# Low parts of two output projections: from a VectorE subtraction to a ScalarE negation and an adding transfer

## The chip, the core and the metric

The kernel runs on one core of one Trainium2 chip. The metric is the device time of one execution in microseconds (us), the median of several runs. Its engines are TensorE (PE; its weight loads are listed apart as PEld), VectorE (DVE), ScalarE (ACT), GpSimd (POOL) and SyncE (SP), which here only issues transfers.

## The reference, cut to what matters

The reference is a decoder trunk of two layers over 512 tokens of 1024 features, in float32. Layer 0 mixes tokens with gated linear recurrences (HGRN2 and retention heads), layer 1 with sparse attention. Each layer then has a SwiGLU network:

```python
for layer in range(DEPTH):
    hn = rmsnorm(h, mix_norm[layer])
    if layer % 2 == 0:
        h = h + even_mixer(hn, ...)      # ends in  o @ even_w_out   (1024 x 1024)
    else:
        h = h + odd_mixer(hn, ...)       # ends in  out @ odd_w_out  (1024 x 1024)
    h = h + swiglu(rmsnorm(h, ffn_norm[layer]), ffn_w_gate_up[layer], ffn_w_down[layer])
return rmsnorm(h, final_norm)
```

The change touches the weights of the two products that end the mixers, `o @ even_w_out` and `out @ odd_w_out`.

## The kernel before, in words

Features lie on the 128 partitions and the 512 tokens along the free dimension. To multiply float32 numbers precisely, each operand is cut into a high part, rounded to the float32r type, and a low part, the rest. A product is then three matmuls into the same PSUM bank (`mm3`, L89 to L91): high by high, high by low, low by high, written `wh` with `xh`, `wh` with `xl`, `wl` with `xh` for a weight `w`.

A weight tile of 128 by 1024 is loaded by SP into one of three buffers `raw` (`load`). `split` treats it in two halves of 512 columns: ACT writes the rounded high part `wh` (L78), and DVE subtracts it from `raw` to give `wl` (L79). There are seven buffers for `wh` and seven for `wl`, each for half a tile, so a cast waits until PE has read the half of seven halves before. A `raw` buffer is free for the next load once both halves are cut.

`ffn` begins with the output projection of the mixer: eight tiles in the order `OUT_ORDER` (0, 4, 1, 5, 2, 6, 3, 7), each of 24 matmuls into a bank `ps_o`. When a tile is done, DVE adds it to the residual `h` (L286), `token_side` forms the sums and differences of the two token halves for a Strassen product and cuts them into high and low parts (names `xg`, `b1`, `b2`, `t1` to `t4`, `tr`; ACT casts at L214, DVE subtractions at L215), and `square` gathers the sum of squares (`sq`, `acc`, L120 and L121). Then come the seven products of the gate and up projections, which need both the token sides of all tiles and the cut sums of four weight blocks (`weight_side`: `sw`, `sh`, `sl`, L259 to L264). The copies `u` (L327, L330, L335) carry partial sums out of PSUM between these products. The first group of the network has no down projection to run between its products.

The order of instructions on each engine is made by the scheduler of the tile framework: it goes by the order of the code as priority and by modelled times. Each engine then takes its instructions strictly in that order, and waits on semaphores that the framework sets. The eight tiles' weights are cast and cut ahead of their use, as far as the buffers allow: in layer 0 during the last projections of the mixer, in layer 1 during the attention.

The change adds `weight_add` beside `weight`, and calls it in `ffn` where `ps_o` is computed.

Of the kernel before, what the change touches and what calls it, by code (L numbers as in the profile page):

```python
# [9 lines left out]
F32 = mybir.dt.float32  # L10
F32R = mybir.dt.float32r
U8 = mybir.dt.uint8
AF = mybir.ActivationFunctionType
ALU = mybir.AluOpType
# [3 lines left out]
P = 128  # L18
# [8 lines left out]
WS = 512  # L27
# [25 lines left out]
class Core:  # L53
# [17 lines left out]
    def split(self, raw, n, pool):  # L71
        nc = self.nc
        out = []
        for o in range(0, n, WS):
            m = min(WS, n - o)
            wh = self.wp.tile([P, WS], F32R, tag="wh", name="wh", bufs=7)
            wl = self.wp.tile([P, WS], F32R, tag="wl", name="wl", bufs=7)
            nc.scalar.copy(wh[:, :m], raw[:, o:o + m])  # L78
            (nc.gpsimd if pool else nc.vector).tensor_tensor(wl[:, :m], raw[:, o:o + m], wh.bitcast(F32)[:, :m],  # L79
                                                             ALU.subtract)  # L80
            out.append((wh, wl))
        return out

# [186 lines left out]
    def ffn(self, outs, w_out, gain, layer, next_gain):  # L270
        tc, nc, io, sp = self.tc, self.nc, self.io, self.sp
        with tc.tile_pool(name="fs", bufs=1) as fs, tc.tile_pool(name="fps", bufs=6, space=PSUM) as fps:
# [4 lines left out]
            for i, m in enumerate(OUT_ORDER):  # L277
                ps = self.bank(self.turn + 1 + i // 3, "ps_o") if i in BANK_OUT else \
                    fps.tile([P, T], F32, tag="gu", name="ps_o")
                w = self.weight(w_out[m])  # L280
                if i == BANK_OUT[1] and self.last is not None:
                    with tc.issue_after(self.last):
                        self.dense_t(ps, w, outs)
                else:
                    self.dense_t(ps, w, outs)
                nc.vector.tensor_tensor(self.h[m], ps, self.h[m], ALU.add)  # L286
                self.token_side(m, gain, kept, b)
                self.square(m, self.h[m], acc)
# [13 lines left out]
            out = []  # L302
# [14 lines left out]
            for size in GROUPS:  # L317
                hid = []
                for j in range(done, done + size):
# [30 lines left out]
                    if before:  # L350
                        n = KD // size
# [809 lines left out]
```

## Time and profile before

| what | value |
|---|---|
| median of 3 runs | 1310.82 us (1310.17 to 1310.92) |
| the profiled execution's own time | 1311.86 us |
| its span, first to last instruction | 1308.9 us |
| outside the span | 2.96 us |
| mean granted TensorE clock | 0.984 |
| busy: PE, PEld, DVE, ACT, POOL | 97%, 86%, 79%, 56%, 25% |
| output projection of layer 0 on PE | 241.7 to 287.6 us, overlapped at its start with the mixer's end |
| output projection of layer 1 on PE | 900.9 to 936.1 us for most of it; a first part is run within the attention |

The busy share of an engine is an average over stages with different limits. The times of the rows are in us from the start of the span. A busy PE is not PE at its peak, since the ends of its pipelined matmuls are modelled.

### The profile page before, as it was taken

The numbers are of one execution on the slowest core, as the hardware profiler recorded it, in microseconds if no ns is written. First come the engines' busy times: TensorE is split into PE (matmuls) and PEld (weight loads), VectorE is DVE, ScalarE is ACT, GpSimd is POOL, SyncE is SP. The second block draws the span as 40 slices with busy tenths as digits, with TensorE's granted clock in tenths as the row PEclk, the third lists the DMA queues.
The fourth block names the chain that finished last, engine by engine and source line by source line (L and its number), as shares of the span: only waits on it lengthen the run. The fifth ranks groups of instructions, "written<-read, shape, count | busy, mean of one in ns | idle before, by whom it ended". The sixth has DMA issues, their size and how long they took to land.

```text
span 1308.9 us, 21707 instructions
## 1 busy us (share of the span) xinstructions
PE 1270.2 (97%) x7846; PEld 1120.7 (86%) x7846; DVE 1028.2 (79%) x2027; ACT 731.7 (56%) x1587; POOL 332.0 (25%) x371
## 2 busy tenths in 40 slices
PE   9999999998999999999988999999989999999995
PEld 7888888888999999999877888887889999999984
DVE  7896764699998887876762789995989888878755
ACT  6655444675554444444554778895755444444444
POOL 3432431001121111111015666762012111111101
PEclk9999999999999999999997999999989999999998
DMA  7212212123233333332322211101223333333321
GB/s 262 84 65 75 72 65 65 65 81 101 85 109 109 107 106 100 100 97 88 104 90 93 78 52 52 44 18 34 85 81 125 105 97 98 97 101 102 105 57 64
DMA packets 44123, 115.10 MB, mean 88 GB/s; under 512 B 4913, under 2 KB 10481, under 8 KB 44017
## 3 DMA queue, kind: packets, MB, share of 16 engines
q1 hardware_dynamic: 43872, 113.69, 27.2%
q8 instruction: 61, 1.00, 0.3%
q14 instruction: 46, 0.37, 0.1%
q10 hardware_dynamic: 144, 0.04, 0.0%
HBM read 111.62 MB, written 2.10 MB: 87 GB/s over the span
## 4 chain that ended last, share of the span: by engine, by line
PE 60%; DVE 8%; issue 2%; DMA 2%; ACT 2%; POOL 1%; DVEq 0%; ACTq 0%; POOLq 0%
PE p L89 9%; PE p L90 9%; PE p L91 9%; PE ps_d L90 5%; PE ps_d L91 5%; PE ps_d L89 5%; DMA raw<-in_gu 2%; PE po L966 2%; PE pt L935 2%; PE ps_o L89 2%; PE ps_o L91 2%; PE ps_o L90 2%; DVE wl L79 1%; PE ps_q L89 1%; PE ps_q L90 1%
## 5 line engine op out<-in xcount | busy, mean ns | idle before, releaser
L78 ACT CAST wh<-raw 128x512 fp32r<-128x512 f32 (+2 forms) x356 | 212.8, 605 | 216.2 <-PE p L90 76.8
L79 DVE TENSOR_TENSOR wl<-raw,wh 128x512 fp32r<-128x512 f32 (+2 forms) x340 | 244.0, 723 | 43.2 <-ACT wh L78 42.1
L214 ACT CAST sh<-sw 128x512 fp32r<-128x512 f32 x176 | 107.6, 618 | 144.4 <-PE p L90 126.4
L341 POOL TENSOR_TENSOR s<-s,rstd 128x256 f32<-128x256 f32 x44 | 38.9, 884 | 510.9 <-DVE s L336 451.7
L215 DVE TENSOR_TENSOR sl<-sw,sh 128x512 fp32r<-128x512 f32 x176 | 146.3, 848 | 6.5 <-ACT sh L214 6.2
L90 PE MATMUL ps_d<-hl,wh 128*128 128x512 f32 x344 | 136.0, 395 | 0.4 <-DVE hl L348 0.2
L91 PE MATMUL ps_d<-hh,wl 128*128 128x512 f32 x344 | 135.6, 394 | 0.0
L89 PE MATMUL ps_d<-hh,wh 128*128 128x512 f32 x344 | 134.5, 396 | 0.6 <-ACT hh L347 0.5
L342 POOL TENSOR_TENSOR g<-g,rstd 128x512 f32<-128x512 f32 x42 | 70.9, 1689 | 138.2 <-DVE g L338 114.5
L259 DVE TENSOR_TENSOR sw<-raw 128x512 f32<-128x512 f32 x44 | 30.3, 689 | 65.3 <-DMA raw<-in_gu 65.2
L91 PEld LDWEIGHTS ps_d<-hh,wl 128*128 128x128 f32 x344 | 64.5, 188 | 14.9
L918 ACT ACTIVATE p<-p,mx 128x256 f32<-128x256 f32 (+3 forms) x128 | 71.6, 564 | 10.1 <-DVE mx L910 9.6
L90 PE MATMUL ps_e<-xl,wh 128*128 128x512 f32 x192 | 76.7, 401 | 0.5 <-DVE xl L109 0.5
L927 POOL TENSOR_SCALAR p<-p,sm 128x128 f32<-128x128 f32 (+3 forms) x128 | 68.6, 554 | 33.2 <-DVE sm L924 15.0
L89 PE MATMUL ps_e<-xh,wh 128*128 128x512 f32 x192 | 76.8, 403 | 0.2
L91 PE MATMUL ps_e<-xh,wl 128*128 128x512 f32 x192 | 76.6, 401 | 0.0
L90 PEld LDWEIGHTS ps_d<-hl,wh 128*128 128x128 f32 x344 | 64.7, 188 | 13.2 <-DVE hl L348 1.0
L89 PEld LDWEIGHTS ps_d<-hh,wh 128*128 128x128 f32 x344 | 64.2, 188 | 13.5 <-ACT hh L347 1.0
L910 DVE CUSTOM_DVE_ANT_0 p<-ps_s,bias 128x256 f32<-128x256 f32 (+3 forms) x128 | 59.0, 481 | 8.1 <-PE pt L935 4.9
L313 DVE TENSOR_TENSOR h<-ps_d,h 128x512 f32<-128x512 f32 x80 | 54.6, 682 | 6.5 <-PE ps_d L91 6.3
L343 ACT ACTIVATE g<-g 128x512 f32<-128x512 f32 x44 | 27.8, 632 | 53.1 <-POOL g L342 52.9
L950 DVE TENSOR_TENSOR pl<-pt,ph 128x512 fp32r<-128x512 f32 (+2 forms) x96 | 51.5, 549 | 5.9 <-ACT ph L942 5.7
(342 smaller groups left out, 4112.8 us busy)
## 6 DMA issues: line engine op xcount, KB each, us to landing
raw<-in_gu SPq DMA_DIRECT2D x88, 512.0 KB, 3.8
raw<-in_dn SPq DMA_DIRECT2D x80, 256.0 KB, 2.7
raw<-in_ein SPq DMA_DIRECT2D x22, 512.0 KB, 3.7
raw<-in_oin SPq DMA_DIRECT2D x12, 512.0 KB, 3.7
raw<-in_eout SPq DMA_DIRECT2D x8, 512.0 KB, 3.8
bias<-in_bias SPq DMA_DIRECT2D x16, 256.0 KB, 2.6
raw<-in_oout SPq DMA_DIRECT2D x8, 512.0 KB, 3.5
h<-in_x SPq DMA_DIRECT2D x8, 256.0 KB, 5.0
```

The lines of the kernel that those rows point to most:

```text
L78: nc.scalar.copy(wh[:, :m], raw[:, o:o + m])
L79: (nc.gpsimd if pool else nc.vector).tensor_tensor(wl[:, :m], raw[:, o:o + m], wh.bitcast(F32)[:, :m], ALU.subtract)
L89: mm(ps, ah, bh, start=start, stop=False, skip_group_check=more)
L90: mm(ps, ah, bl, start=False, stop=False, skip_group_check=more)
L91: return mm(ps, al, bh, start=False, stop=stop, skip_group_check=more)
L214: nc.scalar.copy(hi, src)
L215: nc.vector.tensor_tensor(lo, src, hi.bitcast(F32), ALU.subtract)
L313: nc.vector.tensor_tensor(self.h[m], ps, self.h[m], ALU.add)
L342: (nc.vector if j == NF - 1 else nc.gpsimd).tensor_tensor(g, g, r, ALU.mult)
L910: nc.vector.tensor_tensor_reduce(p, h["dst"][:, b - br[0]], h["bias"][:, T - n:], -1.0, 3e38, ALU.add, ALU.min, h["mx"][:, t, b:b + 1])
L918: nc.scalar.activation(p, p, AF.Exp, bias=h["mx"][:, t, b:b + 1], scale=-1.0, accum_out=h["sm"][:, t, b:b + 1])
L927: nc.gpsimd.tensor_scalar(p, p, h["sm"][:, t, b:b + 1], 1.0, ALU.mult, ALU.mult)
```

## The change

For the sixteen weight tiles of the two output projections, in each of the 32 halves, DVE no longer subtracts. ACT casts the high part as before, then writes minus the high part into `wl`, and POOL issues a transfer from SBUF to SBUF that adds `raw` to `wl` in place. `wl` ends with the same value, raw minus high part.

```diff
+    def weight_add(self, ap):
+        nc = self.nc
+        n = ap.shape[1]
+        raw = self.load(ap)
+        out = []
+        for o in range(0, n, WS):
+            m = min(WS, n - o)
+            wh = self.wp.tile([P, WS], F32R, tag="wh", name="wh", bufs=7)
+            wl = self.wp.tile([P, WS], F32R, tag="wl", name="wl", bufs=7)
+            nc.scalar.copy(wh[:, :m], raw[:, o:o + m])
+            nc.scalar.activation(wl[:, :m], wh.bitcast(F32)[:, :m], AF.Identity, scale=-1.0)
+            nc.gpsimd.dma_start(wl.bitcast(F32)[:, :m], raw[:, o:o + m], accum_op=ALU.add)
+            out.append((wh, wl))
+        return out
...
-                w = self.weight(w_out[m])
+                w = self.weight_add(w_out[m])
```

## Rows read from the trace of the kernel before

**Rows 1.** Page, part 1: busy us (share of the span) xinstructions, by engine.

```profile
PE 1270.2 (97%) x7846; PEld 1120.7 (86%) x7846; DVE 1028.2 (79%) x2027; ACT 731.7 (56%) x1587; POOL 332.0 (25%) x371
```

**Rows 2.** Windows around layer 0's output projection: length, busy by engine, PEclk, DMA.

```profile
261.00:287.00 26.00, 26.00 (x113) 20.92 (x113) 25.98 (x53) 20.87 (x44) 0.00 (x0) 1.00 0.30 100
287.00:310.00 23.00, 18.92 (x129) 17.07 (x128) 22.97 (x49) 12.95 (x29) 0.36 (x1) 0.93 0.21 63
```

**Rows 3.** Windows in layer 1: attention, output projection, start of the network.

```profile
732.00:840.00 108.00, 107.49 (x660) 90.93 (x658) 96.28 (x326) 91.41 (x265) 79.22 (x118) 1.00 0.17 52
...
909.00:918.00 9.00, 9.00 (x41) 7.23 (x40) 8.96 (x20) 7.76 (x17) 0.00 (x0) 1.00 0.33 115
...
943.00:962.00 19.00, 14.54 (x85) 12.84 (x84) 15.58 (x32) 11.99 (x24) 0.73 (x1) 0.82 0.23 77
```

**Rows 4.** Waits of PE, 240 to 310 us: total, times, longest.

```profile
PE p L90 <- DVE t1l L215: 1.0, 1, 1.0
PE p L89 <- ACT u L335: 0.9, 1, 0.9
```

**Rows 5.** Group of ACT by form: busy us, mean ns of one, idle before it.

```profile
L108 ACT ACTIVATE xh<-h,par 128x512 fp32r<-128x512 f32 x16 | 11.3, 721 | 3.2 <-DMA par<-in_par 1.7 <-DMA h<-in_x 1.0 <-PE ps_d L91 0.6
```

**Rows 6.** Transfers by line: count, KB each, median us from issue to landing.

```profile
raw<-in_eout SPq DMA_DIRECT2D x8, 512.0 KB, 3.8
bias<-in_bias SPq DMA_DIRECT2D x16, 256.0 KB, 2.6
...
dec<-in_dec SPq DMA_DIRECT2D x1, 514.0 KB, 6.0
```

**Rows 7.** Timeline of DVE: start us, us, line, operation, out<-in.

```profile
261.62 0.68 DVE L79 TENSOR_TENSOR wl<-raw,wh 128x512 fp32r<-128x512 f32 x1
...
271.25 0.68 DVE L79 TENSOR_TENSOR wl<-raw,wh 128x512 fp32r<-128x512 f32 x1
...
273.40 0.68 DVE L259 TENSOR_TENSOR sw<-raw 128x512 f32<-128x512 f32 x1
...
290.06 0.68 DVE L286 TENSOR_TENSOR h<-ps_o,h 128x512 f32<-128x512 f32 x1
...
912.20 0.68 DVE L79 TENSOR_TENSOR wl<-raw,wh 128x512 fp32r<-128x512 f32 x1
912.80 0.42 DVE L215 TENSOR_TENSOR t3l<-tr,t3h 128x256 fp32r<-128x256 f32 x1
...
917.49 0.68 DVE L79 TENSOR_TENSOR wl<-raw,wh 128x512 fp32r<-128x512 f32 x1
...
937.02 0.68 DVE L286 TENSOR_TENSOR h<-ps_o,h 128x512 f32<-128x512 f32 x1
...
963.68 2.39 DVE L215 TENSOR_TENSOR sl<-sw,sh 128x512 fp32r<-128x512 f32 x2
```

**Rows 8.** Timeline of PE in the two projections and just behind the first.

```profile
246.41 0.63 PE L91 MATMUL ps_o<-oh,wl 128*128 128x512 f32 x2
...
271.08 0.40 PE L91 MATMUL ps_o<-oh,wl 128*128 128x512 f32 x1
...
287.18 0.39 PE L91 MATMUL ps_o<-oh,wl 128*128 128x512 f32 x1
...
288.72 0.28 PE L91 MATMUL p<-t1h,sl 128*128 128x256 f32 x1
...
935.68 0.40 PE L91 MATMUL ps_o<-oh,wl 128*128 128x512 f32 x1
```

**Rows 9.** Timeline of ACT, of SP's queue and of POOL.

```profile
242.09 0.64 ACT L78 CAST wh<-raw 128x512 fp32r<-128x512 f32 x1
...
260.55 1.66 ACT L78 CAST wh<-raw 128x512 fp32r<-128x512 f32 x3 [4.74 <-PE ps_o L90]
...
256.56 0.33 SPq L64 DMA_DIRECT2D raw<-in_eout  x1
...
963.25 1.68 POOL L342 TENSOR_TENSOR g<-g,rstd 128x512 f32<-128x512 f32 x1 [4.55 <-DVE g L338]
```

## The prediction

> **What bounds the kernel now.** I read the page's first part first: PE is busy for 1270.2 us of the span, DVE for 79% of it, ACT for 56%, POOL for 25% [rows 1]. So the time is PE's work plus PE's gaps, and the change takes no work off PE. It can only move gaps. The second view is therefore the windows, to find where PE has gaps near the weights that change, and the third is PE's list of waits there. In layer 0, PE is full from 261 to 287 us, while DVE is too, with 25.98 of 26 us. Then from 287 to 310 us PE is busy for only 18.92 of 23 us while DVE still has no free moment (22.97), and the granted clock averages 0.93 [rows 2]. In layer 1 the same stretch, 943 to 962 us, has PE busy for 14.54 of 19 us at a mean clock of 0.82 [rows 3]. These are gaps of 4.1 and 4.5 us. A mean of 0.93 over 23 us, with levels of 2.4 and 1.2 GHz, means 3.2 us at the lower level, which lose 1.6 us; 0.82 over 19 us means 6.8 us, which lose 3.4 us. So there is at most 4.1 + 1.6 = 5.7 us to get back behind the first projection, and 4.5 + 3.4 = 7.9 us behind the second.
>
> What sets these gaps? PE waits for both kinds of work: 1.0 us for a low part that DVE writes, 0.9 us for a copy that ACT makes between two products [rows 4]. How far DVE lags can be measured at the eighth tile. Its last matmul in layer 0 starts at 287.18 us and lasts 0.39 us [rows 8], but DVE adds the tile to `h` only at 290.06 us [rows 7]: 2.5 us late. In layer 1 the last matmul ends at 935.68 + 0.40 = 936.08 us [rows 8] and the add is at 937.02 us [rows 7]: 0.9 us late. So DVE carries a backlog into the stretch where PE starves, more in layer 0 than in layer 1.
>
> **What is removed.** 32 subtractions of 0.68 us [rows 7], 21.8 us of DVE's busy time. Neighbours overlap: the one at 912.20 us is followed at 912.80 us [rows 7], so each takes 0.60 us of DVE's queue, 19.2 us in all. Only those count that stand in a backlog that PE later feels. In layer 0 that is those from 261.62 to 271.25 us, six of them; in layer 1 those from 912.20 to 917.49 us, four [rows 7]. DVE's queue becomes shorter by 6 x 0.60 = 3.6 us and 4 x 0.60 = 2.4 us. It can't gain more than the lag, because then it waits for PE's tile. I take the smaller of the two each time: 2.5 us and 0.9 us, together 3.4 us. The lower bound is 0, if ACT's copies are what PE waits for; the upper bound is 6.0 us plus the 5.0 us of the slow clock.
>
> **What is added on ACT.** 32 negations from `wh` to `wl`. The nearest row of the same kind, an activation that writes float32r, takes 0.72 us [rows 5]; three casts in a row take 1.66 us, 0.55 us each [rows 9]. So ACT gets 18 to 23 us more. Around the projections there is room: 20.87 of 26 us and then 12.95 of 23 us are busy [rows 2]. In the attention there is little: 91.41 of 108 us [rows 3], and eight of the 32 halves are cut in that window. If all eight stood on the path, that would cost 8 x 0.72 = 5.8 us; DVE loses eight subtractions there, up to 4.8 us to the good. PE is busy for 107.49 of the 108 us, so little of either can reach it. I take +0.4 us.
>
> **What is added on POOL and as transfers.** The trace has no transfer issued by POOL and none that adds, so its cost is bounded. The issue takes between 0.33 us, as on SP's queue, and 1.68 us, POOL's own longest common instruction on a tile of this width [rows 9]; I take 1.0. The landing takes between 2.6 us (256 KB, plain) and 6.0 us (514 KB, the slowest load) [rows 6]. An adding transfer reads two tiles of 256 KB, so I take the 3.8 us of the 512 KB loads [rows 6]. The way from the end of the cast to a finished `wl` is then 0.7 + 1.0 + 3.8 = 5.5 us, with ends of 3.5 and 8.4 us. Now the same way is short: the first of the three casts at 260.55 us [rows 9] ends by 261.17 us, and its `wl` is done at 261.62 + 0.68 = 262.30 us [rows 7], 1.1 us later. So each low part comes about 4.4 us later than now, up to 7.3.
>
> Does PE notice? In the order of the code these casts are those of the sixth tile and of half the seventh. A tile is 24 matmuls at 0.233 us, 5.6 us, and the eighth ends at 287.18 us, so the sixth begins at 270.6 us; its first use of `wl` is the row at 271.08 us [rows 8]. The lead is 271.08 - 262.30 = 8.8 us. That is the shortest lead among the steady tiles of both layers, and even the upper end of 7.3 us fits. Only the tile that fills PE while the last heads finish is tight: the half whose cast runs from 242.09 us for 0.64 us [rows 9] is read by a pair of matmuls that starts at 246.41 us [rows 8]. By the new way it is ready at 242.73 + 5.5 = 248.2 us, 1.8 us late, or 4.7 us at the upper end. Two thirds of this tile's matmuls use the high part alone and can go first, so I take 0.5 us, between 0 and 4.7.
>
> In the Trainium skill, "DMA: Bandwidth & Descriptors", section "Anatomy of one DMA — SWDGE (gpsimd) path", a transfer issued by GpSimd takes 2.0 us plus its bytes at 436 GB/s, which gives an estimate of 2.6 us for 256 KB. No row here shows such a transfer; by that price the way is 1.2 us shorter, and the sum stays as it is, since the lead hides either.
>
> **The buffers.** A `raw` tile is now held until the transfer has landed, so the loads of the gate and up weights start about 4.4 us later. DVE's first sum from them is at 273.40 us [rows 7], and PE reads the low part of that sum at 288.72 us [rows 8], 15 us later, through some 7 us of DVE and ACT work between. That leaves about 8 us of slack: nothing is charged.
>
> **The sum.** -2.5 - 0.9 + 0.4 + 0.5 = -2.5 us. The profiled execution took 1311.86 us, 2.96 us of it outside the span, and so becomes 1309.4 us. It lies 1.04 us above the median of the runs, so I predict a median of 1308.3 us. About 0.2%, 2.6 us, is what a measurement of this kernel can tell from no change; the forecast lies at that edge.
>
> **Rivals.**
> - *Hidden anyway.* PE's gaps are made by the chain product, ACT's copy, next product, which stays as it is, and the added 0.9 us on other engines eat the rest. For it: half of PE's named waits are on ACT [rows 4], and ACT gets more work. Against it: DVE is full through the gap [rows 2]. Time: 1310.8 us. Chance 0.30.
> - *The adding transfer is slow.* If its way takes more than 1.1 + 8.8 = 9.9 us, PE stops in each projection, and the `raw` tiles come late too. With a way of 13 us, each projection loses 3 us, the tight tile some 3 us more, and DVE's gain is gone behind PE: 1310.8 + 9 = 1320 us. For it: nothing in the trace bounds an addition within a transfer. Against it: even 6.0 us of landing is not enough. Chance 0.10.
> - *POOL and DVE get in each other's way.* In the one row where POOL's tensor instruction runs from 963.25 us for 1.68 us [rows 9], two of DVE's subtractions take 2.39 us in place of 1.28 us [rows 7], 1.1 us more. If each issue on POOL did this to DVE, ten in the two backlogs would cost 11 us against 6 us saved: +5 us, 1316 us; it decides from 0.6 us for each issue. Chance 0.07. The Trainium skill, "SBUF — State Buffer", section "Who interferes with whom", says that a DVE instruction with two SBUF inputs contends with a GpSimd instruction that reads SBUF, not with one that only writes it; the row agrees with the first half, and by the second half this rival falls, since the same section infers that the making of descriptors needs the write side only.
> - *The attention pays.* ACT at 85% and POOL at 73% of 732 to 840 us [rows 3] get eight negations and eight issues in their queues; behind an issue that waits for its negation stand the scalings of `p` on POOL, and PE waits for those. At 0.72 us for half of the eight: +2.9 us; with both queues charged, +5. Time 1313 to 1315 us. Chance 0.10.
> - *The forecast*, PE's gaps shrink: 0.43, with 1303 us where the slow clock goes as well.
>
> Of the forecast I count 0.40 as faster by over 0.2% and 0.03 as within; half of the attention's case stays within 0.2% too, since DVE's gain stands against it. So faster is 0.40, same 0.38, slower 0.22. The likeliest case alone reaches from 1303.5 to 1310 us. The range takes in the hidden case and most of the attention's, and leaves out the slow transfer: 1303 to 1315 us.
>
> **What would show it.** DVE's backlog at the eighth tile (2.5 and 0.9 us) should shrink, PE's 18.92 of 23 us and 14.54 of 19 us should rise, ACT should gain 18 to 23 us and DVE lose about 22 us of busy time, and POOL should show 32 transfers that land within 3 to 6 us. PE waits on `wl` in the projections would mean that the leads don't hold; an unchanged gap with an earlier add to `h` would mean that ACT's copies set it. The order of all engines is made anew by the scheduler; a different order of the products could move either gap by a microsecond or two, and that would make the prediction wrong without any of its steps being so.

## Result and profile after

The changed kernel takes 1320.78 us (median of 4 runs, 1318.66 to 1325.09) where the kernel before, beside it, takes 1310.79 us. The ratio is 1.0081 with a 95% interval of 1.0056 to 1.0107: slower by about 10 us. The forecast was 2.5 us faster, and the time lies above the upper end of its range, 1315 us. The profiled execution after took 1320.99 us, 1318.8 us of it the span.

The page after, its busy line, the line of the new queue and the group of the new transfers (count, KB each, median us from issue to landing):

```profile
PE 1269.9 (96%) x7846; PEld 1119.0 (85%) x7846; DVE 1010.6 (77%) x1995; ACT 745.7 (57%) x1619; POOL 356.9 (27%) x403
...
q0 software_dynamic: 4608, 8.39, 3.8%
...
wl<-raw POOLq DMA_DIRECT2D x32, 256.0 KB, 3.5
```

Against [rows 1], PE does the same work (0.3 us less), DVE has 17.6 us less, ACT 14.0 us more and POOL 24.9 us more. So the work moved the way it was meant to, and the 10 us are gaps of PE. The windows after, with the columns of [rows 2], at the same times as before; the work in the last two comes some 2 to 6 us later than it did:

```profile
261.00:287.00 26.00, 26.00 (x113) 20.96 (x112) 19.60 (x42) 22.31 (x46) 5.22 (x6) 1.00 0.66 150
287.00:310.00 23.00, 17.74 (x121) 15.37 (x119) 23.00 (x46) 13.19 (x29) 0.00 (x0) 1.00 0.24 80
943.00:962.00 19.00, 15.29 (x103) 13.78 (x101) 17.80 (x38) 12.87 (x26) 0.00 (x0) 0.91 0.22 67
```

DVE was busy for 25.98 of 26 us while PE ran the projection of layer 0 [rows 2]; now it is busy for 19.60 us. Yet from 287 to 310 us it is as full as before, and PE is busy for less of it, 17.74 us in place of 18.92 us. The time that DVE was given it spent idle, and then it was late. The waits of DVE after, 255 to 300 us (total, times, longest), and its timeline with one row of PE show on what:

```profile
DVE h L302 <- PE ps_o L107: 7.1, 3, 5.7
DVE sw L275 <- DMA raw<-in_gu: 3.1, 1, 3.1
DVE tr L254 <- ACT xg L239: 1.6, 2, 0.8
```

```profile
276.02 0.42 DVE L245 TENSOR_TENSOR tr<-xg 128x256 f32<-128x256 f32 x1
279.51 0.69 DVE L275 TENSOR_TENSOR sw<-raw 128x512 f32<-128x512 f32 x1 [3.07 <-DMA raw<-in_gu]
...
282.60 0.68 DVE L302 TENSOR_TENSOR h<-ps_o,h 128x512 f32<-128x512 f32 x1
...
289.62 0.69 DVE L302 TENSOR_TENSOR h<-ps_o,h 128x512 f32<-128x512 f32 x1
...
293.30 0.68 DVE L302 TENSOR_TENSOR h<-ps_o,h 128x512 f32<-128x512 f32 x1
```

```profile
288.97 0.40 PE L107 MATMUL ps_o<-oh,wl 128*128 128x512 f32 x1
```

The seventh tile's addition before:

```profile
284.84 0.68 DVE L286 TENSOR_TENSOR h<-ps_o,h 128x512 f32<-128x512 f32 x1
```

The first sum of the gate and up weights starts at 279.51 us; before, it was at 273.40 us [rows 7]. DVE stood 3.07 us for its load, and everything behind it in DVE's queue stood too: the seventh tile's addition to `h` comes at 289.62 us in place of 284.84 us. The eighth tile's last matmul ends at 288.97 + 0.40 = 289.37 us and its addition is at 293.30 us, 3.9 us late, where the backlog was 2.5 us [rows 7, 8]. Behind the second projection DVE stands for the same load again, for 1.5 us (waits of DVE, 885 to 965 us):

```profile
DVE sw L275 <- DMA raw<-in_gu: 1.5, 1, 1.5
```

Why the load is late stands in the waits of SP's queue after, 225 to 300 us:

```profile
SPq L64 <- DMA wl<-raw: 44.0, 5, 13.8
SPq L267 <- DMA wl<-raw: 17.0, 3, 5.9
```

Three loads of gate and up weights (L267) waited for a transfer that still read the `raw` buffer. The first of them was issued at 268.34 us, before at 263.53 us, 4.8 us later. DVE's first sum, though, adds the two halves of the second weight tile, and the load of that one is 7.2 us later. Its issue before, and then after:

```profile
267.54 0.33 SPq L251 DMA_DIRECT2D raw<-in_gu  x1
```

```profile
274.72 0.33 SPq L267 DMA_DIRECT2D raw<-in_gu  x1
```

So the delay grows from load to load. The loads of the projection's own tiles (L64) wait for such transfers too, 44.0 us in all.

A second thing is seen in the two programs: SP's order is the same, but the scheduler issues some 1,200 of PE's 7,503 instructions, 460 of DVE's and 250 of ACT's at another place than before, most of them in the attention and in the two networks. So there are two suspects: what the new work does (either the held `raw` tile, or the late low parts and ACT's extra work), and the new order. The texts put on record before the runs give the letters A and B to theories anew in each group of runs, and say each time what they stand for.

**Where each kernel loses.** Each matching DVE instruction gives a lag: its start in one trace less its start in the other, less the same difference at 47.5 us. One profiled execution stands behind each line of this table, so single lags can be off by a microsecond or so. The instants are those of the kernel before: the seventh tile's addition in layer 0, the end of layer 0, the attention, the eighth tile's addition in layer 1, the last addition to `h` in the final stage.

| kernel, against | 285 us | 648 us | 842 us | 937 us | 1296 us |
|---|---|---|---|---|---|
| changed, before | 4.4 | 4.2 | 5.7 | 6.0 | 9.1 |
| add_oldorder, before | 8.0 | 7.2 | 4.7 | 11.0 | 9.0 |
| sub_hold, before | 8.1 | 7.7 | 7.5 | 13.3 | 13.3 |
| sub_neworder, before | 1.6 | 0.0 | 4.7 | 3.8 | 4.3 |
| sub_new1, before | 0.0 | -0.8 | 4.3 | 3.3 | 4.2 |
| neg_neworder, before | 2.6 | 2.2 | 6.5 | 5.1 | 6.8 |
| sub_old_raw4, before | 0.0 | -3.4 | -5.3 | -6.3 | -5.9 |
| add_old_raw4, sub_old_raw4 | 3.9 | 5.0 | 4.6 | 6.1 | 4.7 |
| add_late_raw4, sub_old_raw4 | 0.8 | 2.1 | 3.4 | 4.6 | 1.8 |

### The profile page after: what moved, and what is told of

Its sections match the earlier page's. It is cut to its first block, busy times and chain, and to the rows that moved or that the text cites. A ratio compares the mean times of both kernels' runs of the same rounds, so it can differ in the third digit from the quotient of the medians.

```text
span 1318.8 us, 21769 instructions
## 1 busy us (share of the span) xinstructions
PE 1269.9 (96%) x7846; PEld 1119.0 (85%) x7846; DVE 1010.6 (77%) x1995; ACT 745.7 (57%) x1619; POOL 356.9 (27%) x403
## 4 chain that ended last, share of the span: by engine, by line
PE 65%; DVE 16%; DMA 7%; ACT 5%; issue 4%; POOL 2%; SPq 0%; DVEq 0%; ACTq 0%; POOLq 0%
PE p L105 7%; PE p L106 6%; DMA raw<-in_gu 6%; PE p L107 6%; PE ps_d L106 4%; PE ps_d L107 4%; PE ps_d L105 4%; PE ps_e L105 3%; PE ps_e L106 3%; DVE wl L79 3%; PE ps_e L107 3%; PE po L982 2%; DVE sl L231 2%; PE pt L951 2%; PE ps_o L105 2%
## 5 line engine op out<-in xcount | busy, mean ns | idle before, releaser
L78 ACT CAST wh<-raw 128x512 fp32r<-128x512 f32 (+2 forms) x324 | 192.8, 603 | 173.0 <-PE p L106 65.5
L79 DVE TENSOR_TENSOR wl<-raw,wh 128x512 fp32r<-128x512 f32 (+1 forms) x308 | 218.2, 715 | 33.1 <-ACT wh L78 32.6
L934 ACT ACTIVATE p<-p,mx 128x512 f32<-128x512 f32 (+3 forms) x128 | 71.5, 563 | 10.9 <-DVE mx L926 10.6
L943 POOL TENSOR_SCALAR p<-p,sm 128x128 f32<-128x128 f32 (+3 forms) x128 | 68.0, 551 | 20.9 <-DVE sm L940 13.3
L926 DVE CUSTOM_DVE_ANT_0 p<-ps_s,bias 128x512 f32<-128x512 f32 (+3 forms) x128 | 58.5, 484 | 12.9 <-PE pt L951 7.0
```

What stands on the lines that cost most here:

```text
L926: nc.vector.tensor_tensor_reduce(p, h["dst"][:, b - br[0]], h["bias"][:, T - n:], -1.0, 3e38, ALU.add, ALU.min, h["mx"][:, t, b:b + 1])
L934: nc.scalar.activation(p, p, AF.Exp, bias=h["mx"][:, t, b:b + 1], scale=-1.0, accum_out=h["sm"][:, t, b:b + 1])
L943: nc.gpsimd.tensor_scalar(p, p, h["sm"][:, t, b:b + 1], 1.0, ALU.mult, ALU.mult)
```

## Experiments

Several kernels issue a written order: a list of positions for each engine, taken from one of the two programs, is imposed by edges that fix the order of issue and wait for nothing. The instructions that only one of the two has are left out of the list and placed by the scheduler. The cuts of code below leave out the bookkeeping for that (`self.extra`).

```diff
+            pin(self)
...
+        for x, y in zip(order, order[1:]):
+            tc.add_manual_dep(l[y], l[x].name, info(), reason="pin")
```

**New work or new order: add_oldorder, sub_neworder.** The first has the changed kernel's operations in the order of the kernel before; the second puts the subtraction back and keeps the changed kernel's order:

```diff
-            nc.scalar.activation(wl[:, :m], wh.bitcast(F32)[:, :m], AF.Identity, scale=-1.0)
-            nc.gpsimd.dma_start(wl.bitcast(F32)[:, :m], raw[:, o:o + m], accum_op=ALU.add)
+            nc.vector.tensor_tensor(wl[:, :m], raw[:, o:o + m], wh.bitcast(F32)[:, :m], ALU.subtract)
```

> The changed kernel's instructions, but every engine issues the instructions that both kernels have in the order of the kernel before; only the 32 negations and the 32 transfers are placed anew. Theory A, the 10 us come from the new order of the products and their helpers that the scheduler made: 1307 to 1311 us, and PE's gaps in both networks are as in the kernel before. Theory B, they come from the new work itself (ACT's negations, the transfers, raw tiles held longer): 1317 to 1322 us.

> The instructions of the kernel before (DVE subtracts), but every engine issues those that both kernels have in the order of the changed kernel; only the 32 subtractions are placed anew. Theory A, the order costs the time: 1316 to 1322 us. Theory B, the new work costs it: 1309 to 1313 us. Between them: both pay a part, and the two kernels give the shares.

add_oldorder: 1321.77 us, ratio 1.0083 (1.0064 to 1.0102). sub_neworder: 1317.81 us, 1.0044 (1.0027 to 1.0061). Both suspects cost time, and the two don't add up: the work alone costs 11 us in the old order, the order alone some 6 us with the old work, and both together 10 us. The lags say why. In the old order the work loses 8 us at the first projection (the lag is 3.1 us just before DVE's first sum and 8.0 us at it) and 6.3 us more at the second. The new order gives up 4.7 us in the attention, and in it the new work loses only 2.8 us at the first projection (4.4 less 1.6), 4.2 us by the end of layer 0 and 4.8 us by the end (9.1 less 4.3). In add_oldorder the waits of DVE, 255 to 300 us and then 900 to 960 us, and those of PE, 236 to 320 us, are:

```profile
DVE sw L275 <- DMA raw<-in_gu: 4.8, 1, 4.8
```

```profile
DVE sw L275 <- DMA raw<-in_gu: 6.7, 1, 6.7
```

```profile
PE ps_o L107 <- DMA wl<-raw: 2.5, 2, 1.7
```

DVE's first sum waits for its load behind both projections, and PE waits for low parts in layer 0 alone.

**One layer at a time: add_layer0, add_layer1.** `weight_add` is called in one layer and `weight` in the other, and the scheduler is free.

```diff
-                w = self.weight_add(w_out[m])
+                w = (self.weight_add if layer == 0 else self.weight)(w_out[m])
```

> The change in layer 0's output projection alone, scheduled freely. Theory B, costs that stay with the work: the changed kernel was 4.2 us behind at the end of layer 0, so 1310.8 + 4.2 = 1315 us. Theory A: the order is made anew once more, so anything from 1308 to 1320 us, and the two kernels with one layer each don't add up to 10 us.

> The change in layer 1's output projection alone, scheduled freely. Theory B: the changed kernel lost another 5 us or so from the attention to the end of layer 1, so 1310.8 + 5.5 = 1316 us. Theory A: 1308 to 1320 us, and layer 0, which this kernel leaves as it was, gives time away or wins it wherever its order differs.

add_layer0: 1320.53 us, 1.0071 (1.0048 to 1.0094). add_layer1: 1315.87 us, 1.0037 (1.0023 to 1.0050). Together that is 14 us, more than the 10 us of the change. Layer 0 alone cost twice what I expected: its lag is 4.3 us at the end of layer 0, as in the changed kernel, 6.8 us at 1285 us and 9.6 us at 1296 us, so more than half of it arises in layer 1 and in the final stage, which have none of the new work. These two runs only say that the projections can't be priced apart while the order is free.

**The held raw tile by itself: sub_hold.** DVE subtracts as before, in the old order, and POOL then issues a transfer that adds `wl` to `raw`, where nothing reads it:

```diff
             nc.vector.tensor_tensor(wl[:, :m], raw[:, o:o + m], wh.bitcast(F32)[:, :m], ALU.subtract)
+            nc.gpsimd.dma_start(raw[:, o:o + m], wl.bitcast(F32)[:, :m], accum_op=ALU.add)
```

> The kernel before in its own order, with DVE's subtractions, and behind each of the 32 a transfer issued by POOL that adds the low part to the raw tile, which nothing reads any more. It holds the raw tile and loads the transfer queue as the change does, but the low part comes at its old time and ACT has no extra work. Theory A now, the raw tile that is held until the transfer lands makes the loads of the gate and up weights late, and DVE, which waits for them at the head of its queue, keeps the token sides waiting: 1317 to 1323 us, with a wait of DVE's first sum for the load of 3 to 7 us behind both projections. Theory B, late low parts and ACT's negations cost the time: 1309 to 1313 us.

It took 1321.71 us, 1.0083 (1.0067 to 1.0099): as much as add_oldorder, with no work for ACT and no low part that waits for a transfer. DVE's waits in this kernel, 236 to 315 us and then 885 to 965 us:

```profile
DVE sw L276 <- DMA raw<-in_gu: 4.6, 1, 4.6
```

```profile
DVE sw L276 <- DMA raw<-in_gu: 6.4, 1, 6.4
```

These are the waits of add_oldorder (4.8 and 6.7 us), and at these two sums the lag grows by 4.7 and 6.0 us (in add_oldorder by 4.9 and 6.4 us). But not all of the loss is the same. A lag of 3.4 us is there before the first sum, and it comes from a wait that add_oldorder doesn't have: one of DVE's subtractions stands for 3.20 us, where before it stood for 0.90 us. The row of sub_hold, then of the kernel before:

```profile
251.64 0.69 DVE L95 TENSOR_TENSOR wl<-raw,wh 128x512 fp32r<-128x512 f32 x1 [3.20 <-ACT gate L715]
```

```profile
249.60 0.69 DVE L79 TENSOR_TENSOR wl<-raw,wh 128x512 fp32r<-128x512 f32 x1 [0.90 <-ACT wh L78]
```

The ACT instruction named has nothing to do with this tile; an added transfer landed at the same moment, and the subtraction has a semaphore of the added transfers among its waits. In add_oldorder some 3 us are lost up to there as well, but there PE waits for low parts. The added transfer also loads the DMA queue and POOL, so this run doesn't yet prove that holding is the cause; the fourth buffer below does for the old order.

**A fourth raw buffer: add_old_raw4, sub_old_raw4, add_raw4, and later sub_raw4.** The names tell operation and order: in the first two the old order is written down, in the others the scheduler is free.

```diff
-        raw = self.wp.tile([P, WN], F32, tag="raw", name="raw", bufs=3)
+        raw = self.wp.tile([P, WN], F32, tag="raw", name="raw", bufs=4)
...
-        tr = lambda: fs.tile([P, TH], F32, tag="tr", name="tr", bufs=7)
+        tr = lambda: fs.tile([P, TH], F32, tag="tr", name="tr", bufs=6)
```

> The negations and transfers of the change in the order of the kernel before, with four raw buffers in place of three (and six in place of seven for the differences tr, to make room). Theory A (raw held): the loads no longer wait for the transfers, so of the 11 us some 2.5 stay, PE's wait for the low parts of the tile that fills: 1310 to 1315 us. Theory B (late low parts, ACT): 1318 to 1323 us, as with three buffers.

> The control: the kernel before in its own order, with the same four raw buffers and six tr. By both theories 1308 to 1312 us, as before; if the fourth buffer itself helps, that shows here, and the run with the transfers is read against this one.

> The changed kernel, scheduled freely, with four raw buffers and six tr. By theory A for layer 0 its 4 to 5 us there go away; what its own order costs in layer 1 stays: 1312 to 1317 us. By theory B 1318 to 1322 us.

> The kernel before, scheduled freely, with four raw buffers and six tr: the control for the changed kernel with four buffers (1311.5 us), and what the buffer is worth without an order written down. By theory A 1303 to 1309 us, below that kernel; if the scheduler's new order costs more than the buffer gives, 1310 to 1316 us.

The first three came out below the ranges expected, by 0.8, 2.8 and 0.5 us, and sub_raw4 at 1309.79 us between its two.

| | DVE subtracts | ACT and the transfer |
|---|---|---|
| three buffers, old order | 1 (the kernel before) | 1.0083 (1.0064 to 1.0102) |
| four buffers, old order | 0.9962 (0.9950 to 0.9973), 1305.16 us | 0.9992 (0.9982 to 1.0003), 1309.16 us |
| four buffers, free order | 0.9989 (0.9978 to 1.0000), 1309.79 us | 1.0012 (1.0001 to 1.0022), 1311.52 us |

With the same transfers and the same traffic, one more buffer takes the cost of the work in the old order from 11 us to 0.9992 - 0.9962 = 0.0030, 4 us (2 us to either side). What is left is another wait. PE's waits on `ps_o`, 236 to 315 us, and POOL's issue of the transfer in question, both of add_old_raw4:

```profile
PE ps_o L107 <- DMA wl<-raw: 3.3, 2, 1.7
```

```profile
246.94 0.86 POOL L96 DMA_DIRECT2D wl<-raw  x1 [0.83 <-ACT wl L95]
```

```profile
248.60 0.50 PE L107 MATMUL ps_o<-oh,wl 128*128 128x512 f32 x1 [1.67 <-DMA wl<-raw]
...
253.26 0.50 PE L107 MATMUL ps_o<-oh,wl 128*128 128x512 f32 x1 [1.59 <-DMA wl<-raw]
```

Both waits are for the fourth tile, which fills PE while the last heads finish. DVE no longer waits for a load there, and behind the second projection for 0.5 us. The control, sub_old_raw4, beats both kernels: the fourth buffer is worth 0.4% to the kernel before where its order is kept, and 0.1%, at the edge of what can be told, where the scheduler makes a new one. In the free orders the work costs 0.0023, 3 us, with four buffers, but there the order differs too.

**DVE's relief without its price: add_late_raw4.** As add_old_raw4, but the first four tiles of each projection are cut by DVE:

```diff
-                w = self.weight_add(w_out[m])
+                w = self.weight_add(w_out[m], i > 3)
```

> Order of the kernel before, four raw buffers, six tr; the last four tiles of each output projection get their low parts by negation and transfer, the first four by DVE as before. PE's waits for low parts in layer 0 concerned the fourth tile, so they should be gone, and raw tiles no longer hold up the loads: only the good side of the change is left, 16 subtractions less on DVE, those in the backlog among them. If DVE's backlog is what PE waits for behind the projections, as the forecast had it: up to 3.4 us under the control with four buffers (1305.2 us), so 1302 to 1303.5 us. If the relief of DVE reaches nothing: 1304.5 to 1306.5 us.

It took 1306.81 us, 0.9974 (0.9962 to 0.9986), against 0.9962 (0.9950 to 0.9973) for the control: no gain, and 0.3 us above the range expected if the relief reaches nothing. Negations and transfers of the last four tiles are still there, so this is the net. The windows of the control and then of this kernel:

```profile
261.00:287.00 26.00, 26.00 (x113) 20.97 (x112) 25.85 (x52) 22.00 (x46) 0.00 (x0) 1.00 0.29 100
287.00:310.00 23.00, 18.59 (x139) 16.95 (x138) 23.00 (x49) 12.28 (x27) 0.22 (x1) 1.00 0.18 63
```

```profile
261.00:287.00 26.00, 26.00 (x113) 20.96 (x112) 21.48 (x44) 24.11 (x50) 5.20 (x6) 1.00 0.71 167
287.00:310.00 23.00, 18.45 (x123) 16.55 (x122) 23.00 (x48) 13.39 (x29) 0.00 (x0) 0.93 0.19 61
```

DVE has 4.4 us less to do up to 287 us and is exactly as full behind it. The additions of the eighth tile and the matmuls before them, of the control and then of this kernel:

```profile
290.15 0.72 DVE L302 TENSOR_TENSOR h<-ps_o,h 128x512 f32<-128x512 f32 x1
```

```profile
287.31 0.40 PE L107 MATMUL ps_o<-oh,wl 128*128 128x512 f32 x1
```

```profile
291.32 0.68 DVE L306 TENSOR_TENSOR h<-ps_o,h 128x512 f32<-128x512 f32 x1
```

```profile
288.20 0.39 PE L111 MATMUL ps_o<-oh,wl 128*128 128x512 f32 x1
```

The backlog is 290.15 - 287.71 = 2.4 us in the control and 291.32 - 288.59 = 2.7 us here. Eight subtractions less, and it did not shrink. (The clock of 0.93 in the last window is of one profiled execution.)

**Where the order costs: sub_new1.** The kernel before with the old order up to the end of layer 0 and the changed kernel's order from there on.

> DVE subtracts, three raw buffers; the order of the kernel before up to the end of layer 0, that of the changed kernel from there on (the attention, its projection, layer 1's network). If the new order's 6 to 7 us come from the attention, as the lags of the kernel with the whole new order say: 1314.5 to 1318 us. If they come from layer 0: 1309 to 1312 us.

It took 1317.26 us, 1.0056 (1.0037 to 1.0076), as much as the whole new order within the intervals. Its lag grows from -0.8 to 4.3 us between 648 and 842 us. PE's waits, 690 to 1020 us:

```profile
PE ps_s L918 <- DVE mx L926: 2.1, 5, 1.0
PE pt L951 <- DVE sm L940: 1.1, 1, 1.1
```

Before, PE waited 0.2 us for the maxima and not for this scaling. Products of the projection and of the heads stand in another order, and in it PE meets DVE's maxima and scalings before they are done: 3.0 us of the 5.1 us, by these waits.

**ACT's part within the changed order: neg_neworder.** ACT negates as in the changed kernel, and DVE adds in place of the transfer:

```diff
-            nc.gpsimd.dma_start(wl.bitcast(F32)[:, :m], raw[:, o:o + m], accum_op=ALU.add)
+            nc.vector.tensor_tensor(wl[:, :m], raw[:, o:o + m], wl.bitcast(F32)[:, :m], ALU.add)
```

> The changed kernel's own order, with ACT's 32 negations, but DVE adds the raw tile to the negated high part in place of the transfer: no transfer, the raw tile is free some 3 us earlier than in the changed kernel, ACT's extra work stays and DVE's relief goes. If the transfers (raw held, low parts late) are what the new work costs within the changed kernel: about the time of the kernel with this order and plain subtractions (ratio 1.0044), 1314.5 to 1318 us, and layer 0 without the changed kernel's 4 us of lag. If ACT's negations cost it: 1319 to 1322 us, with that lag.

It took 1318.11 us, 1.0055 (1.0035 to 1.0074), between sub_neworder's 1.0044 and the changed kernel's 1.0081; the intervals overlap on both sides. The lag at the end of layer 0 is 2.2 us, half of the changed kernel's 4.2 us; had the transfers been all of it, none was expected. But the half can't be put down to ACT in the changed kernel: here it is DVE that adds, and DVE stands for the negations, 236 to 315 us, where in the changed kernel POOL does:

```profile
DVE wl L96 <- ACT wl L95: 4.7, 3, 4.3
```

So this run leaves the shares of the transfers and of ACT open. What it shows is that DVE no longer waits for the first sum's load (the sum starts at 278.35 us with no idle time before it).

## Why the prediction was wrong

**The step that failed: the buffers, charged at nothing.** I had seen that `raw` would be held 4.4 us longer and put the loads that much later. That was too little: 4.8 us for the first load, 7.2 us for the second, which the first sum needs. I then took 15 us from DVE's first sum to PE's read of its low part, less 7 us of work, as slack. That counts the delay along the sum's own chain. But DVE takes its instructions in order, and behind the first sum stand the additions to `h` and the token sides of the last tiles, which PE needs first. The slack was that of the sum itself: its load was issued at 267.54 us before and, at the 3.8 us of a 512 KB load [rows 6], had landed by about 271.3 us (an estimate), 2 us before the sum at 273.40 us. DVE had no free moment in that stretch [rows 2], so what it stood for the load became backlog. At the eighth tile of layer 0, reckoned as in the prediction, the backlog is 2.5 us in the kernel before, 7.6 us in add_oldorder (298.64 less 291.02), 7.1 us in sub_hold (297.87 less 290.74), and 2.7 us in add_old_raw4 (294.02 less 291.31), which keeps the transfers and has a fourth buffer. In the changed kernel's own order it is 3.9 us, and 289.89 - (288.73 + 0.39) = 0.8 us in sub_neworder, which has that order and subtracts. Its rows:

```profile
289.89 0.69 DVE L302 TENSOR_TENSOR h<-ps_o,h 128x512 f32<-128x512 f32 x1
```

```profile
288.73 0.39 PE L107 MATMUL ps_o<-oh,wl 128*128 128x512 f32 x1
```

These 3.1 us more are what DVE stood for its load there (3.07 us). In the time of the run the held buffer is worth 7 of the 11 us in the old order (11 with three buffers, 4 with four).

**The second step: the order, put at a microsecond or two.** The last section had named it as something that could make the prediction wrong without any of its steps being so. It had no term in the sum, and it cost about 6 us: sub_neworder loses 0.44% with none of the new work.

**The gain of 2.5 and 0.9 us did not come.** DVE's backlog at the eighth tile was right as a measurement, and wrong as something that earlier work on DVE could shorten. The subtractions that went stand before 272 us; in the time they left DVE waited for PE's tiles, for ACT, for a load. The 23 us behind 287 us, where DVE stays full, hold the token sides and the cuts of the gate and up weights, and with the relief alone they did not begin earlier: in add_late_raw4 the first sum starts at 274.66 us, in its control at 273.51 us. In the changed kernel the backlog is 3.9 and 943.40 - (941.68 + 0.40) = 1.3 us; forecast were 0 and 0. The rival "hidden anyway" had this part right: of PE's waits for the copies `u` behind the first projection, the longest stays at 0.9 us in the changed kernel, as it was before [rows 4].

**What was right, or nearly.** DVE lost 17.6 us of busy time and ACT gained 14.0 us; about 22 and 18 to 23 had been forecast. POOL's issue takes 0.87 us (1.0 assumed), the landing 3.2 to 6.7 us with a median of 3.5 (3.8 assumed). From the end of the cast to the wait's end it is 4.7 us in add_oldorder (5.5 assumed): the cast of the half that PE first waits for ends at 244.36 us, and PE goes on at 249.08 us. The Trainium skill, "DMA: Bandwidth & Descriptors", section "Anatomy of one DMA — SWDGE (gpsimd) path", would give an estimate of 2.6 us for the landing; the median here is 0.9 us above it, counted from the start of POOL's issue, and the same 2.6 us counted from its end. The leads of the steady tiles held, and no wait for `wl` is among PE's waits in the changed kernel. That the fourth tile is tight was right, but its term was too small: 0.5 us in the sum, 2.5 and 3.3 us in the two runs with the old order; the second wait of add_old_raw4 is for one slow transfer, since PE goes on at 253.26 us, 6.3 us after the issue at 246.94 us began. In the changed kernel the scheduler moved that tile's reads, and the wait is gone. One reading was off without harm: 287.18 us is where the eighth tile's last matmul starts, not where it ends (287.57 us), so the lead was no shorter than reckoned.

**The rivals.** The transfer was not slow, yet the side effect named under that rival, `raw` tiles that come late, was there at a way of half its threshold: it needed a chance of its own. That the time is the 1320 us of this rival is chance, since about half of it is the new order. POOL and DVE did not disturb each other: DVE's instructions on 512 columns beside the seven issues between 259 and 276 us take 0.68 to 0.69 us, as before. The attention did pay, 2.7 us of lag from 724 to 842 us in the changed kernel, but not by its queues: sub_new1 pays more there with no negation and no transfer, and in add_oldorder the attention gives 1.5 us back. It is the order.

**What stays open.** Why lag grows again within the networks, from 1.7 us at 314 us to 4.2 us at 648 us and by 3 us behind 937 us in the changed kernel, and by 5 us in add_layer0's untouched last part (where PE waits for squares of ACT, 4.2 us from 1280 to 1320 us), no run here separates. Nor does one separate ACT's negations from the transfers in the changed kernel's own order. It isn't known which of the moved products makes the attention slower. And the cost in the changed kernel's own order is only bounded: about 5 us for the new work (1.0081 less 1.0044 is 4.9 us), about 6 us for the order (0.0044), with some 4 and 2 us to either side.

## What to carry to other kernels

When a step is moved to a slower path, price the buffer that it reads as carefully as the value that it writes: the holder's end is the next load's start, and that load's first reader may stand at the head of an in-order queue whose engine is already full. There the slack is only the time from the load's landing to that reader (2 us here), however far off the reader's own consumer is. And where a scheduler remakes the order, run the old work in the new order and the new work in the old one before you explain a difference by the work.

## What the runs showed that was not expected

A transfer from SBUF to SBUF that adds in place takes 3.2 to 6.7 us for 256 KB, median 3.5 with its issue, and a plain load of 256 KB in this kernel takes 2.6 [rows 6]; the issue holds POOL for 0.87 us. One more 4 KB a partition for the load buffer is worth 5 us to the kernel before in its own order, though PE's list of waits around the projection [rows 4] names no load. Another place for some 2,000 instructions of the same work costs 6 us.
